# Delta rule: substitution on blocks of 16 with a compact merge, and the convolution's sums in PSUM

## Chip, cores and metric

The kernel runs on one core of a Trainium2 chip. The metric is the device time of one execution in microseconds (us); of the kernel before, three runs took 1975.92 to 1977.36 us, with a median of 1976.27 us.

## What is computed

The program is one step of a two-layer backbone for 128 context tokens and 512 latent tokens of width 1024. Layer 0 is a state-space mixer beside neighbourhood attention, layer 1 a bidirectional gated delta rule; both have an MLP. Only layer 1's mixer is touched. For each of 8 heads and each direction it does, on chunks of tokens:

```
qkv  = silu(dwconv(h @ w_in, conv_w))            # 5 taps along the tokens
q, k = q / |q| * dk**-0.5,  k / |k|
A    = tril(beta k k^T * decay, -1);   Tm = inv(I + A)
u, w = Tm @ (beta v),  Tm @ (beta k exp(gcum))
per chunk:  v_new = u - w @ S
            o     = (q exp(g)) @ S + (tril(q k^T) * decay) @ v_new
            S     = S exp(g_last) + (k exp(g_last - g))^T @ v_new
out  = (rmsnorm(o_fwd + o_bwd) * silu(z)) @ w_out
```

## The kernel before

All 640 tokens go together: 128 context tokens and 512 latent ones, in five chunks of 128 (chunk 0 is the context). Heads are handled in four pairs, P0 to P3, and one pair has both directions, so four units of 128 x 128 per chunk.

For a pair, `gdn_project` multiplies the normalised stream by six weight columns, m = 0 to 5 (k, k, q, q, v, v for the two heads). Each column is 2 halves x 8 x 3 = 48 matmuls of 320 columns (L205 to L207), 288 in a pair, and goes through `ev`: ScalarE copies it out of PSUM into `cb` (two buffers), the five taps are summed into `cv` (three buffers) by VectorE (L1322), a tanh and a last multiplication make it silu. After m = 1, `squares(0)`, `tok(0)` and `normalize` follow for the keys: squares summed on TensorE (L1272), a root in several small VectorE operations that begins at L1274 and ends at L182, transposition (L1299), multiplication (L1278), transposition back (L1285). After m = 3 come the squares of the queries, after m = 5 the transposed values. These use the PSUM tag `pc`, which hands out its banks in program order.

The squares stand in a tile of their own, `tsq`, with one buffer. The end of a chain (L1655, L1671) uses another tag with one buffer, `osq`, for the squares of its output and for the row of scales, which a DMA (`or`<-`osq`) writes out.

From m = 2 on, `gdn_group` runs once for each of the five chunks: decay factors (POOL L1376, ACT L1379), the product of the keys (L1394 and L1395), its evacuation (L1400), and DMAs that lay the 32 x 32 diagonal blocks of A as rows of `ub`, 80 rows of 1024. `gdn_blocks` inverts all 80 blocks at once by substitution, 31 steps of two VectorE operations (L1425 multiplies, L1427 subtracts).

`gdn_inverse` then builds the inverse of the 128 x 128 units. It spreads the blocks to block-diagonal tiles `gD` and `gTT` (POOL multiplies by a mask, L1453; VectorE transposes, L1454) and merges blocks of 32 to 64 and 64 to 128 with matmuls that have 128 rows and 32 or 64 columns (L1458). `gdn_chain` walks the chunks: t = 0 for the context, then t = 1 to 4, each with a step that depends on the state of the one before: TensorE L1615, VectorE L1620, TensorE L1625, ScalarE L1627, TensorE L1631/L1632 and L1643, VectorE L1646. It ends with L1655 to L1671.

In `odd` the program order is: project P0, P1, solve P0 (inverse and chain), P2, solve P1, P3, solve P2, then the projection of z and solve P3. A scheduler arranges each engine's instructions before the run into one fixed queue, from priorities (the chain and the inverse are the most urgent, then the substitution, then the groups) and its own estimates; DMAs are all issued by SP, in one queue. So an engine whose next instruction waits does nothing else. The gemm with `wouto` follows, and the scales of the last chain are used first at L1699.

Of the kernel before, what the change touches and what calls it, by code (L numbers as in the profile page):

```python
# [11 lines left out]
F32 = mybir.dt.float32  # L12
# [8 lines left out]
T = 640  # L21
# [127 lines left out]
class Build:  # L149
# [1098 lines left out]
    def gdn_project(self, pr, hn, P, first=None, mid=None):  # L1248
# [13 lines left out]
        def squares(ty):  # L1262

            p = self.ps("pc")
            for hh in range(2):
                for c0, c1 in ((0, 3), (3, 5)):
                    sq = P.tile([128, 4, 128], F32, name="tsq", bufs=1)
                    nc.scalar.activation(sq[:, :c1 - c0].rearrange("p a b -> p (a b)"),
                                         out[2 * ty + hh][:, 128 * c0:128 * c1], AF.Square)
                    for c in range(c0, c1):  # L1270
                        i = 2 * c + hh
                        nc.tensor.matmul(p[:, 2 * i:2 * i + 2], sq[:, c - c0], self.ones2, start=True, stop=True)  # L1272
            ssq = self.sp.tile([128, 10], F32, name="ssq", tag="ssq", bufs=2)
            V.tensor_scalar(ssq, p[:, 0:20:2], EPS, None, op0=AD)  # L1274
            return self.rsqrt(self.sp, ssq, 10, "l2n").rearrange("p (c h) -> p c h", h=2)
# [18 lines left out]
        def tok(ty):  # L1294
            for part in range(3):
                p = self.ps("pc")
                jobs = [(c, part) for c in range(1, 5)] if part < 2 else [(0, 0), (0, 1)]
                for i, (c, hh) in enumerate(jobs):
                    nc.tensor.transpose(p[:, 128 * i:128 * i + 128], out[2 * ty + hh][:, 128 * c:128 * c + 128], self.ident)  # L1299
                n = len(jobs)  # L1300
                pv = p.rearrange("p (a b) -> p a b", a=4)[:, :n]
                dst = ktok if ty == 0 else vtok
                if part < 2:
                    nc.scalar.activation(dst[part][:, 1:5], pv, AF.Copy)
                else:
                    for hh in range(2):
                        V.tensor_copy(dst[hh][:, 0], pv[:, hh])
        def ev(m, h, p):
# [9 lines left out]
            cv = self.tl([128, 642], "cv")  # L1318
            nc.scalar.activation(cv, cb[m][:, 0:642], AF.Identity, scale=cw[:, 0:1])  # L1319
            split = m > 3 and pr > 0  # L1320
            for t in range(1, 4 if split else 5):
                V.scalar_tensor_tensor(cv, cb[m][:, t:t + 642], cw[:, t:t + 1], cv, op0=M, op1=AD)  # L1322
            if split:
                cy = cb[m][:, 4:646]
                nc.scalar.activation(cy, cy, AF.Identity, scale=cw[:, 4:5])
                nc.gpsimd.tensor_tensor(cv, cv, cy, op=AD)
            th = cb[m][:, 0:642]
            nc.scalar.activation(th, cv, AF.Tanh)

            if m in (2, 3):  # L1330
                nc.scalar.activation(th, th, AF.Identity, bias=1.0)
                nc.gpsimd.tensor_tensor(cv[:, 0:128], th[:, 0:128], cv[:, 0:128], op=M)
                nc.gpsimd.tensor_tensor(cv[:, 128:T], th[:, 130:642], cv[:, 130:642], op=M)
            else:
                V.scalar_tensor_tensor(cv[:, 0:128], th[:, 0:128], 1.0, cv[:, 0:128], op0=AD, op1=M)
                V.scalar_tensor_tensor(cv[:, 128:T], th[:, 130:642], 1.0, cv[:, 130:642], op0=AD, op1=M)
# [78 lines left out]
    def gdn_blocks(self, pr, ub, P):  # L1415
# [3 lines left out]
        D = ub  # L1419
        V.memset(D.rearrange("p a b -> p (a b)")[:, 0:1024:33], 1.0)  # L1420
        tmp = P.tile([80, 256], F32, name="sbt", bufs=1)
        for j in range(31):
            n, m = 31 - j, j + 1
            t = tmp[:, :n * m].rearrange("p (a b) -> p a b", b=m)
            V.tensor_tensor(t, ub[:, j, j + 1:32].unsqueeze(2).to_broadcast([80, n, m]),  # L1425
                            D[:, j, 0:m].unsqueeze(1).to_broadcast([80, n, m]), op=ALU.mult)
            V.tensor_tensor(D[:, j + 1:32, 0:m], D[:, j + 1:32, 0:m], t, op=ALU.subtract)  # L1427
            if j < 30:
                tmp = P.tile([80, 256], F32, name="sbt", bufs=1)
# [4 lines left out]
    def gdn_inverse(self, pr, ud, dd, P):  # L1434
# [3 lines left out]
        cm = P.tile([128, 20, 32], F32, name="gcm")  # L1438
        nc.sync.dma_start(out=cm, in_=self.ap(dd, 0, [[32, 128], [4096, 20], [1, 32]]))
# [5 lines left out]
        mask = self.cst[:, 404:532].rearrange("p (b j) -> p b j", b=4).unsqueeze(1).to_broadcast([128, 2, 4, 32])  # L1445

        D = P.tile([128, 5, 4, 128], F32, name="gD")
        TT = P.tile([128, 5, 4, 128], F32, name="gTT", bufs=2)
        two = lambda t, c, d: t[:, c, 2 * d:2 * d + 2].rearrange("p u j -> p (u j)")
        for c in range(5):  # L1450
            for d, a, b in ((0, D, TT), (1, TT, D)):
                src = cm[:, 4 * c + 2 * d:4 * c + 2 * d + 2].unsqueeze(2).to_broadcast([128, 2, 4, 32])
                G.tensor_tensor(a[:, c, 2 * d:2 * d + 2].rearrange("p u (b j) -> p u b j", b=4), src, mask, op=ALU.mult)  # L1453
                V.transpose(two(b, c, d), two(a, c, d))  # L1454
        CH = [(c, hh) for c in range(5) for hh in range(2)]

        def mm(out, l, r, col):
            nc.tensor.matmul(out, l, r, start=True, stop=True, tile_position=(0, col))  # L1458

        def bank(n):  # L1460
            return self.ps("pb")[:, :320].rearrange("p (c h j) -> p c h j", c=5, h=2)


        p = bank(0)
        for c, hh in CH:
# [6 lines left out]
        pD, pT = bank(0), bank(0)
        for c, hh in CH:
            mm(pD[32:64, c, hh], TT[:, c, hh, 32:64], X[:, c, hh], 32)
            mm(pD[64:96, c, hh], TT[:, c, 2 + hh, 64:96], X[:, c, hh], 64)
        ACT.activation(D[32:64, :, 0:2, 0:32], pD[32:64], AF.Copy, scale=-1.0)
        ACT.activation(D[64:96, :, 2:4, 96:128], pD[64:96], AF.Copy, scale=-1.0)
        for c, hh in CH:
            for a in (0, 64):
                x, y = slice(a, a + 32), slice(a + 32, a + 64)  # L1480
                mm(pT[x, c, hh], X[:, c, hh], TT[:, c, hh, y], a)
                mm(pT[y, c, hh], X[:, c, hh], TT[:, c, 2 + hh, x], a + 32)
        for a in (0, 64):
            x, y = slice(a, a + 32), slice(a + 32, a + 64)
            ACT.activation(TT[x, :, 0:2, y], pT[x], AF.Copy, scale=-1.0)
            ACT.activation(TT[y, :, 2:4, x], pT[y], AF.Copy, scale=-1.0)

        x, y = slice(0, 64), slice(64, 128)
        Y = cm.rearrange("p (c h a) j -> p c h (a j)", c=5, h=2)
        parts = ((0, 4), (4, 5))  # L1490
        for c0, c1 in parts:
            p = self.ps("pb").rearrange("p (c h j) -> p c h j", c=4, h=2)
            for c in range(c0, c1):
                for hh in range(2):
                    mm(p[y, c - c0, hh], uo[:, 0, c, hh, 32:96], D[:, c, hh, x], 64)
                    mm(p[x, c - c0, hh], uo[:, 1, c, hh, 0:64], D[:, c, 2 + hh, y], 0)
            ACT.activation(Y[:, c0:c1], p[:, :c1 - c0], AF.Copy)
        for c0, c1 in parts:
            p = self.ps("pb").rearrange("p (c h j) -> p c h j", c=4, h=2)
            for c in range(c0, c1):  # L1500
                for hh in range(2):
                    mm(p[x, c - c0, hh], Y[:, c, hh], TT[:, c, hh, y], 0)
                    mm(p[y, c - c0, hh], Y[:, c, hh], TT[:, c, 2 + hh, x], 64)
            ACT.activation(TT[x, c0:c1, 0:2, y], p[x, :c1 - c0], AF.Copy, scale=-1.0)
            ACT.activation(TT[y, c0:c1, 2:4, x], p[y, :c1 - c0], AF.Copy, scale=-1.0)
        for c in range(5):
# [4 lines left out]
            else:  # L1511
# [8 lines left out]
                cR=("tsq", 1), cS=("cb", 2))  # L1520

    def gdn_chain(self, pr, pd, TT, P, roles, bank):
# [14 lines left out]
        def load(c):  # L1537

            if c not in held:
# [3 lines left out]
                held[c] = [a[k][:, i] for k in range(2) for i in range(4)]  # L1543
            return held[c]

        def prep(t):
# [9 lines left out]
            if t:  # L1556
# [9 lines left out]
                for u in range(4):  # L1566
                    nc.gpsimd.tensor_tensor(gq[:, u], gq[:, u], lds[u][2 + u % 2], op=M)
# [138 lines left out]
    def odd(self, hn, P, fillers, xd):  # L1706
# [22 lines left out]
        def blocks(pr, pd):  # L1729
            ub = P.tile([80, 32, 32], F32, name="ub", bufs=2)  # L1730
# [43 lines left out]
        zt = P.tile([128, 4, T], F32, name="gD")  # L1774
# [3 lines left out]
        for m in range(4):  # L1778
            o = ot[:, m] if m < 3 else P.tile([128, T], F32, name="gcm")
# [3 lines left out]
        zt = P.tile([128, 4, T], F32, name="gD")  # L1783
# [214 lines left out]
```

## Time and profile before

| | |
|---|---|
| median of three runs | 1976.27 us |
| profiled execution | 1976.35 us, of it 1974.1 us of span |
| TensorE busy | 1799.6 us (91%) |
| VectorE busy | 1290.8 us (65%) |
| ScalarE busy | 869.5 us (44%) |
| GpSimd busy | 760.8 us (39%) |

Layer 1's mixer lies between about 906 and 1475 us of the span. The digits of the page are tenths of busy time in slices of 49.4 us, so this stretch is slices 19 to 30. Times in the rows are microseconds from the start of the span.

### The profile page before, as it was taken

To read this page: it belongs to the slowest core of one execution; us is meant where nothing else is said; L and a number is where in the kernel's file an instruction comes from. 1 tells how busy PE (TensorE), PEld (TensorE's weight loads), DVE (VectorE), ACT (ScalarE), POOL (GpSimd) and SP (SyncE) were. 2 spreads that over 40 slices of the span, in tenths; PEclk is the share of its full clock that TensorE was granted. 3 is DMA by queue.
4 is the path that set the end of the run, shared out by engine and by line. 5 is a ranking of instruction groups with operands and counts; after the bars stand their busy time and mean duration, and the time that the engine had idled before them with its cause. 6 is when DMAs were issued, how large, how long until landed. Compare 5 with 4: busy or idle time off the path is not lost. (4 is left out here: it accounts for less than half of the span.)

```text
span 1974.1 us, 35755 instructions
## 1 busy us (share of the span) xinstructions
PE 1799.6 (91%) x13556; PEld 1698.3 (86%) x13556; DVE 1290.8 (65%) x2825; ACT 869.5 (44%) x1928; POOL 760.8 (39%) x609
## 2 busy tenths in 40 slices
PE   5889889998999999998877889889989899999998
PEld 3789677988999999998877788787878899999997
DVE  8999777369264544548589988774667927364553
ACT  4333356344244353536454455344324425344362
POOL 2622101442343433453455555522235334343451
PEclk9999999998999999998998999898989999999999
DMA  8446886524332222332576478758834122222231
GB/s 319 131 112 169 239 246 228 195 106 140 124 112 84 76 86 75 135 123 78 158 207 196 117 197 238 222 166 267 279 131 149 54 97 76 86 76 86 76 96 54
DMA packets 206985, 286.61 MB, mean 145 GB/s; under 512 B 54879, under 2 KB 138237, under 8 KB 206813
## 3 DMA queue, kind: packets, MB, share of 16 engines
q1 hardware_dynamic: 206812, 284.33, 45.6%
q8 instruction: 107, 1.75, 0.4%
q14 instruction: 66, 0.53, 0.1%
HBM read 228.87 MB, written 46.82 MB: 140 GB/s over the span
## 5 line engine op out<-in xcount | busy, mean ns | idle before, releaser
L196 POOL TENSOR_TENSOR wlo<-raw,whi 128x1024 fp32r<-128x1024 f32 (+1 forms) x153 | 360.8, 2361 | 512.6 <-ACT whi L194 466.6
L194 ACT ACTIVATE whi<-raw 128x1024 fp32r<-128x1024 f32 (+1 forms) x153 | 153.2, 1002 | 324.5 <-PE pg L206 146.6
L207 PE MATMUL pg<-hidh,wlo 128*128 128x320 f32 (+2 forms) x576 | 178.8, 311 | 0.5 <-POOL wlo L196 0.5
L205 PE MATMUL pg<-hidh,whi 128*128 128x320 f32 (+2 forms) x576 | 179.0, 311 | 0.0
L206 PE MATMUL pg<-hidl,whi 128*128 128x320 f32 (+2 forms) x576 | 178.9, 311 | 0.0
L205 PE MATMUL pg<-h10h,whi 128*128 128x320 f32 x472 | 158.9, 337 | 17.5 <-DVE cb L1722 6.5
L422 DVE SCALAR_TENSOR_TENSOR x<-pg,mod,x 128x128 f32<-128x128 f32 (+2 forms) x132 | 53.7, 436 | 179.5 <-PE pg L207 179.5
L206 PE MATMUL pg<-h10l,whi 128*128 128x320 f32 x472 | 155.9, 330 | 0.0
L207 PE MATMUL pg<-h10h,wlo 128*128 128x320 f32 x472 | 155.3, 329 | 0.0
L205 PE MATMUL pa<-hidh,whi 128*128 128x320 f32 x448 | 138.0, 310 | 0.5 <-ACT whi L194 0.5
L207 PE MATMUL pa<-hidh,wlo 128*128 128x320 f32 x448 | 138.4, 309 | 0.0
L206 PE MATMUL pa<-hidl,whi 128*128 128x320 f32 x448 | 138.2, 309 | 0.0
L422 DVE SCALAR_TENSOR_TENSOR x<-pa,mod,x 128x128 f32<-128x128 f32 (+2 forms) x108 | 43.8, 435 | 136.8 <-PE pa L207 136.8
L507 POOL TENSOR_TENSOR wq<-S,wq 128x512 fp32r<-128x512 f32 x52 | 71.3, 1371 | 114.4 <-ACT wq L506 114.4
L205 PEld LDWEIGHTS pg<-h10h,whi 128*128 128x128 f32 x472 | 95.9, 203 | 21.4 <-DVE cb L1722 7.2
L207 PEld LDWEIGHTS pg<-hidh,wlo 128*128 128x128 f32 x576 | 108.2, 188 | 1.6 <-POOL wlo L196 1.0
L205 PEld LDWEIGHTS pg<-hidh,whi 128*128 128x128 f32 x576 | 108.3, 188 | 0.9 <-issue 0.8
L206 PEld LDWEIGHTS pg<-hidl,whi 128*128 128x128 f32 x576 | 108.2, 188 | 0.4 <-DVE hidl L568 0.3
L1322 DVE SCALAR_TENSOR_TENSOR cv<-cb,cw,cv 128x642 f32<-128x642 f32 x90 | 94.6, 1052 | 9.8 <-ACT cv L1319 8.9
L206 PEld LDWEIGHTS pg<-h10l,whi 128*128 128x128 f32 x472 | 95.9, 203 | 0.6 <-issue 0.4
L207 PEld LDWEIGHTS pg<-h10h,wlo 128*128 128x128 f32 x472 | 95.6, 203 | 0.2
L205 PEld LDWEIGHTS pa<-hidh,whi 128*128 128x128 f32 x448 | 83.9, 188 | 2.0 <-ACT whi L194 1.2
(742 smaller groups left out, 5754.2 us busy)
## 6 DMA issues: line engine op xcount, KB each, us to landing
raw<-in_wff SPq DMA_DIRECT2D x104, 512.0 KB
mraw<-in_wmod SPq DMA_DIRECT2D x96, 512.0 KB
raw<-in_wino SPq DMA_DIRECT2D x33, 512.0 KB
rawx<-in_wff SPq DMA_DIRECT2D x24, 512.0 KB
raw<-in_wine SPq DMA_DIRECT2D x16, 512.0 KB
cka<-pd SPq DMA_DIRECT2D x28, 256.0 KB
ckb<-pd SPq DMA_DIRECT2D x28, 256.0 KB
s5g<-s5g SPq DMA_DIRECT2D x32, 164.0 KB
```

Source lines behind the costliest of these rows:

```text
L194: nc.scalar.activation(hi[:, :kt], raw[:, :kt], AF.Copy)
L196: (nc.vector if self.lov and self.nw % self.lov else nc.gpsimd).tensor_tensor(lo[:, :kt], raw[:, :kt], hi[:, :kt], op=ALU.subtract)
L205: nc.tensor.matmul(p[:, :n], hi[:, k], xh[:, s], start=(k == 0), stop=False)
L206: nc.tensor.matmul(p[:, :n], hi[:, k], xl[:, s], start=False, stop=False)
L207: nc.tensor.matmul(p[:, :n], lo[:, k], xh[:, s], start=False, stop=(k == kt - 1))
L422: nc.vector.scalar_tensor_tensor(x[m][:, s], p[:, ls], g, x[m][:, s], op0=ALU.mult, op1=ALU.add)
L507: (V if j % 2 else nc.gpsimd).tensor_tensor(t[:, 4:8], src, t[:, 0:4], op=SU)
L1322: V.scalar_tensor_tensor(cv, cb[m][:, t:t + 642], cw[:, t:t + 1], cv, op0=M, op1=AD)
```

## The change

Four things change in layer 1's mixer, and one of them brings a shared buffer.

The substitution works on blocks of 16: both halves of each block of 32 are handled by one operation, 15 steps of two operations on 30 to 128 elements a row instead of 31 steps on 31 to 256. It writes into a new tile, `ubd`, which GpSimd clears.

The inverse gets a level more, 16 to 32. Blocks stay compact (`gDc`, `gTc`: 128 rows, 32 columns a block); the matmuls take 32 or 64 rows as well as 32 or 64 columns of the array. The level 16 to 32 is 160 matmuls of 32 x 32 a pair, in two rounds of 80, with an evacuation between them. Masks and the block-wise transpositions go; the blocks are copied to their places by ScalarE.

The convolution is done in two parts, 128 tokens in SBUF and 512 in a bank of `pc`, with all sums and the last multiplication on VectorE. GpSimd and ScalarE had a share of these before.

The product of the queries with their decay (L1567) moves from GpSimd to VectorE, in two operations instead of four.

To make room, `squares` and the last pair's chain use the tag `osq` instead of `tsq`, `ub` has one buffer instead of two, and some later tiles take other tags. The core of the diff:

```diff
@@ squares
-                    sq = P.tile([128, 4, 128], F32, name="tsq", bufs=1)
+                    sq = self.tl([128, 5, 128], "osq")
@@ conv, called by ev
+            cv = self.tl([128, 642], "cv")
+            cl = self.ps("pc")
+            parts = ((cv[:, 0:128], 0), (cl, 130))
+            for o, c0 in parts:
+                nc.scalar.activation(o, x[:, c0:c0 + o.shape[1]], AF.Identity, scale=cw[:, 0:1])
+            for t in range(1, 5):
+                for o, c0 in parts[::-1]:
+                    V.scalar_tensor_tensor(o, x[:, c0 + t:c0 + t + o.shape[1]], cw[:, t:t + 1], o, op0=M, op1=AD)
...
@@ gdn_blocks
-        for j in range(31):
-            n, m = 31 - j, j + 1
...
+        D = P.tile([80, 32, 32], F32, name="ubd", bufs=1)
+        nc.gpsimd.memset(D, 0.0)
...
+        for j in range(15):
+            n, m = 15 - j, j + 1
+            sh = [80, 2, n, m]
...
@@ gdn_inverse
-                G.tensor_tensor(a[:, c, 2 * d:2 * d + 2].rearrange("p u (b j) -> p u b j", b=4), src, mask, op=ALU.mult)
-                V.transpose(two(b, c, d), two(a, c, d))
+        px = [bank() for d in range(2)]
+        for d in range(2):
+            for n in range(10):
+                for r in S:
+                    mm(px[d][r, n], Gc[r, d, n], Dc[r, d, n], r.start, r.start)
+            ACT.activation(Xc[:, d], px[d], AF.Copy)
...
+                    mm(px[d][r, n], Tc[r, d, n], Xc[r, d, n], r.start, r.start)
+            V.tensor_tensor(Dc[:, d], Dc[:, d], px[d], op=ALU.subtract)
+            V.transpose(fl(Tc[:, d]), fl(Dc[:, d]))
...
@@ gdn_chain
-                for u in range(4):
-                    nc.gpsimd.tensor_tensor(gq[:, u], gq[:, u], lds[u][2 + u % 2], op=M)
+                for d in range(2):
+                    V.tensor_tensor(gq[:, 2 * d:2 * d + 2], gq[:, 2 * d:2 * d + 2], lds[2 * d][8], op=M)
```

The fixed queues change with it. On TensorE, the place where P2's keys are normalised (`ktok`, L1285) stood among gemm matmuls (`pg`):

```order
L206 MATMUL pg<-h10l_8978,whi 128x320
L207 MATMUL pg<-h10h_8977,wlo 128x320
L1285 MATMUL pc<-cst,ktok 128x128 x4
L205 MATMUL pg<-h10h_8979,whi 128x320
L1285 MATMUL pc<-cst,ktok 128x128 x4
L206 MATMUL pg<-h10l_8980,whi 128x320
L207 MATMUL pg<-h10h_8979,wlo 128x320
```

Now the same place stands behind the end of P0's chain. L1689 is the chain's sum of squares, L1700 the transposition of its scales; L1272, L1299 and L1285 belong to P2's keys, L1394 to its five groups:

```order
L1689 MATMUL pa<-cst,osq 128x2 x5
L1601 MATMUL pa<-cka 128x128 x4
L1700 MATMUL pa<-cst,osc 10x128
L1272 MATMUL pc<-cst,osq 128x2 x3
L1299 MATMUL pc<-cst,cv 128x128 x4
L1272 MATMUL pc<-cst,osq 128x2 x2
L1299 MATMUL pc<-cst,cv 128x128 x4
L1272 MATMUL pc<-cst,osq 128x2 x3
L1299 MATMUL pc<-cst,cv 128x128 x2
L1272 MATMUL pc<-cst,osq 128x2 x2
L1285 MATMUL pc<-cst,ktok 128x128 x10
L1394 MATMUL pb<-khT 128x128 x10
```

P0's inverse and chain stand about one pair earlier among the gemm matmuls than before, and the keys of P2 follow the chain's end with no gemm matmul between them. From the second half of the chain's step t = 2 up to L1394 no L205 to L207 stands in the queue. Nearly the same stands once more at P1's chain and P3's keys.

On ScalarE, in the queue before, the last squares of P3 (`tsq`, the last row with L1268) stood ahead of the end of P0's chain (L1655):

```order
L1268 ACTIVATE tsq<-cv 128x256
L1510 ACTIVATE gTT<-gTT,gcol 128x128 x4
L1313 ACTIVATE cb<-pg 128x128
L1314 ACTIVATE cb<-pg 128x192
L1579 ACTIVATE ckd<-ckb,gkd 128x128 x2
L1655 ACTIVATE osq<-otok 128x640
L1562 ACTIVATE cgq<-cgq 128x512
L1655 ACTIVATE osq<-otok 128x640
```

Now the end of P0's chain (L1686, L1702) stands ahead of the first squares of P2's keys, all in one tag:

```order
L1686 ACTIVATE osq<-otok 128x640 x2
L1593 ACTIVATE cgq<-cgq 128x512
L1702 ACTIVATE osq<-pa 10x128
L1268 ACTIVATE osq<-cv 128x384
L1268 ACTIVATE osq<-cv 128x256
L1304 ACTIVATE ktok<-pc 128x512
L1268 ACTIVATE osq<-cv 128x384
L1304 ACTIVATE ktok<-pc 128x512
L1268 ACTIVATE osq<-cv 128x256
L1315 ACTIVATE cv<-cb,cw 128x128
```

P0's chain has moved ahead of two pairs' squares in this queue.

## Rows read from the trace of the kernel before

**Rows 1.** The page: sums by engine, and 40 slices.
```profile
PE 1799.6 (91%) x13556; PEld 1698.3 (86%) x13556; DVE 1290.8 (65%) x2825; ACT 869.5 (44%) x1928; POOL 760.8 (39%) x609
...
DVE  8999777369264544548589988774667927364553
```
**Rows 2.** Timeline of VectorE: start, duration, engine, line; the keys' normalisation.
```profile
962.87 1.56 DVE L1278 TENSOR_TENSOR ktok<-ktok,l2n_y 128x640 f32<-128x640 f32 x2
...
1021.56 1.55 DVE L1278 TENSOR_TENSOR ktok<-ktok,l2n_y 128x640 f32<-128x640 f32 x2
...
1102.21 1.54 DVE L1278 TENSOR_TENSOR ktok<-ktok,l2n_y 128x640 f32<-128x640 f32 x2
...
1182.24 2.10 DVE L1278 TENSOR_TENSOR ktok<-ktok,l2n_y 128x640 f32<-128x640 f32 x2
```
**Rows 3.** Busy time between these starts, then PEclk, DMA share, GB/s.
```profile
963.00:1022.00 59.00, 48.69 (x332) 47.40 (x333) 41.16 (x78) 31.82 (x72) 30.02 (x35) 0.94 0.82 235
1022.00:1102.00 80.00, 61.26 (x390) 58.97 (x390) 76.83 (x141) 35.96 (x76) 45.00 (x41) 0.91 0.55 159
1102.00:1182.00 80.00, 68.50 (x703) 65.47 (x702) 74.07 (x154) 43.57 (x102) 47.09 (x50) 0.92 0.64 173
1182.00:1475.00 293.00, 260.74 (x2539) 236.40 (x2537) 194.69 (x539) 119.72 (x278) 112.09 (x127) 0.93 0.72 221
```
**Rows 4.** Waits of TensorE, 1022 to 1475 us: total us, times, longest.
```profile
PE pc L1299 <- DVE cv L1336: 6.7, 2, 6.3
```
**Rows 5.** Timeline of TensorE: the last chain's scales.
```profile
1475.41 1.33 PE L1699 MATMUL pc<-cst,osc 128*128 128x128 f32 x5 [2.93 <-DVE osc L1666]
```
**Rows 6.** Groups by line, 900 to 1475 us: busy us, mean ns, idle before.
```profile
L1322 DVE SCALAR_TENSOR_TENSOR cv<-cb,cw,cv 128x642 f32<-128x642 f32 x90 | 94.6, 1052 | 9.8 <-ACT cv L1319 8.9 <-DMA pd<-khT 0.5
L1427 DVE TENSOR_TENSOR ub<-ub,sbt 80x31 f32<-80x31 f32 (+15 forms) x124 | 72.5, 584 | 1.6
L1425 DVE TENSOR_TENSOR sbt<-ub 80x31 f32<-80x31 f32 (+15 forms) x124 | 65.2, 526 | 3.0 <-DMA ub<-utd 1.2
...
L1400 DVE TENSOR_TENSOR gau<-pb,gbg 128x512 f32<-128x512 f32 x20 | 13.4, 681 | 5.5 <-ACT gbg L1379 4.9 <-DMA ckb<-pd 0.6
...
L1335 DVE SCALAR_TENSOR_TENSOR cv<-cb,cv 128x128 f32<-128x128 f32 x16 | 4.5, 284 | 1.6 <-ACT cb L1328 1.3
```
**Rows 7.** Groups of GpSimd, the same stretch.
```profile
L1567 POOL TENSOR_TENSOR cgq<-cgq,cka 128x128 f32<-128x128 f32 x64 | 31.5, 519 | 82.5 <-DVE cgl L1565 50.1 <-DMA cka<-pd 19.3 <-DVE ogn_t L180 7.6
```
**Rows 8.** Busy time of L1458 alone in two inverses (PE, PEld, PEclk).
```profile
1182.00:1218.00 36.00, 8.61 (x280) 6.49 (x280) 0.91 0.89 257
...
1277.00:1310.00 33.00, 7.33 (x280) 5.71 (x280) 1.00 0.54 159
```
**Rows 9.** Timeline of TensorE: runs of L1458 with 32 columns.
```profile
1189.87 0.45 PE L1458 MATMUL pb<-gD,guf 128*32 128x32 f32 x30
...
1199.40 1.02 PE L1458 MATMUL pb<-gcm,gTT 128*32 128x32 f32 x34
```
**Rows 10.** Timeline of TensorE: two gemm matmuls, and four matmuls of a chain.
```profile
1077.61 0.31 PE L206 MATMUL pg<-h10l,whi 128*128 128x320 f32 x1
1077.76 0.31 PE L207 MATMUL pg<-h10h,wlo 128*128 128x320 f32 x1
...
1310.32 1.06 PE L1643 MATMUL pa<-cR,ckd 128*128 128x128 f32 x8
```
**Rows 11.** Timeline: two steps of P2's chain.
```profile
1391.57 1.12 DVE L1620 SCALAR_TENSOR_TENSOR cR<-pa,gneg,ckb 128x128 f32<-128x128 f32 x4
...
1402.92 1.13 DVE L1620 SCALAR_TENSOR_TENSOR cR<-pa,gneg,ckb 128x128 f32<-128x128 f32 x4 [0.33 <-PE pa L1615]
```
**Rows 12.** Timeline of ScalarE: the end of P0's chain.
```profile
1220.68 0.73 ACT L1655 ACTIVATE osq<-otok 128x640 f32<-128x640 f32 x1
...
1259.61 0.27 ACT L1671 ACTIVATE osq<-pa 10x128 f32<-10x128 f32 x1 [1.20 <-PE pa L1669]
```
**Rows 13.** Timeline of VectorE: the root of P2's key squares begins.
```profile
1094.65 0.16 DVE L1274 TENSOR_SCALAR ssq<-pc 128x10 f32<-128x10 f32 x1
```

More of the change, by code (lines that the diff above doesn't have):

```diff
@@ L1317, in ev @@
             cw = self.cw[:, 6 * pr + m]
[L1318 to L1336, printed above, removed]
+            cv = conv(cb[m], cw)
             out[m] = cv
@@ L1455, in gdn_inverse @@
[L1455 to L1465, printed above, removed]
+        D64 = P.tile([128, 10, 64], F32, name="gD64")
+        G.memset(TT, 0.0)
+        G.memset(D64, 0.0)
+        fl = lambda t: t.rearrange("p n j -> p (n j)")
@@ new lines, in gdn_inverse, with mm, bank @@
+        V.transpose(fl(Tc[:, 0]), fl(Dc[:, 0]))
+        V.transpose(fl(Dc[:, 1]), fl(Tc[:, 1]))
+        def mm(out, l, r, row, col):
+            nc.tensor.matmul(out, l, r, start=True, stop=True, tile_position=(row, col))
+        def bank():
+            return self.ps("pb")[:, :320].rearrange("p (n j) -> p n j", n=10)
+        S = [slice(32 * k, 32 * k + 32) for k in range(4)]
+        px = [bank() for d in range(2)]
[4 more added lines that the diff above has]
+            ACT.activation(Xc[:, d], px[d], AF.Copy)
@@ new lines, in gdn_inverse @@
+        px = [bank() for d in range(2)]
+        for d in range(2):
+            for n in range(10):
+                for r in S:
+                    mm(px[d][r, n], Tc[r, d, n], Xc[r, d, n], r.start, r.start)
+            V.tensor_tensor(Dc[:, d], Dc[:, d], px[d], op=ALU.subtract)
+            V.transpose(fl(Tc[:, d]), fl(Dc[:, d]))
+        u2 = lambda d: slice(2 * d, 2 * d + 2)
+        ch = lambda t: t.rearrange("p (c h) j -> p c h j", h=2)
+        for d in range(2):
+            for r in S:
+                ACT.activation(TT[r, :, u2(d), r], ch(Tc[r, d]), AF.Copy)
+            for k in range(2):
+                r = S[2 * d + k]
+                ACT.activation(D64[r, :, 32 * k:32 * k + 32], Dc[r, d], AF.Copy)
@@ L1466, in gdn_inverse @@
+        p = bank()
+        for n in range(10):
+            c, hh = divmod(n, 2)
             for a in (0, 64):
                 x, y = slice(a, a + 32), slice(a + 32, a + 64)
-                mm(p[y, c, hh], uo[:, 0, c, hh, a:a + 32], D[:, c, hh, x], a + 32)
-                mm(p[x, c, hh], uo[:, 1, c, hh, a:a + 32], D[:, c, 2 + hh, y], a)
-        X = cm[:, :10].rearrange("p (c h) j -> p c h j", c=5)
+                mm(p[y, n], uo[x, 0, c, hh, a:a + 32], Dc[x, 0, n], a, a + 32)
+                mm(p[x, n], uo[y, 1, c, hh, a:a + 32], Dc[y, 1, n], a + 32, a)
@@ L1471, in gdn_inverse @@
+        X = Gc[:, 0]
         ACT.activation(X, p, AF.Copy)
[L1472 to L1478, printed above, removed]
+        pD, pT = bank(), bank()
+        for n in range(10):
+            mm(pD[32:64, n], Tc[32:64, 0, n], X[32:64, n], 32, 32)
+            mm(pD[64:96, n], Tc[64:96, 1, n], X[64:96, n], 64, 64)
@@ L1490, in gdn_inverse @@
[L1490 to L1505, printed above, removed]
+        Y = Xc.rearrange("p d n j -> p (d n j)").rearrange("p (n j) -> p n j", n=10)
```

83 lines of the change are left out of this document (54 added, 29 removed).

## The prediction

> **What bounds the kernel now.** I read the page first: TensorE is busy 91% of the span, and VectorE's digits rise to 9 and 8 only at the start and in slices 20 to 24, which is the delta rule [rows 1]. So the question is which engine sets the pace there. As milestones I take the normalisation of each pair's keys, because each pair passes it once, in order: 962.9, 1021.6, 1102.2 and 1182.2 us [rows 2]. The pairs are thus 58.7, 80.6 and 80.0 us apart. From the last to the use of the last chain's scales at 1475.4 us [rows 5] it is 293.2 us, and 499 us follow that the change does not touch. The busy table between these milestones shows VectorE at 77 and 74 us of 80 in the second and third stretch, against 41 of 59 in the first and 195 of 293 in the last, while TensorE has 61 and 68.5 of 80 [rows 3]. VectorE sets the pace in the second and third stretch; in the last TensorE is busy 261 of 293. The waits show how it reaches TensorE: once it stood 6.3 us for the last multiplication of a convolution [rows 4], work that had queued on VectorE.
>
> **What the change removes.** The substitution costs 72.5 + 65.2 = 137.7 us in 248 operations, 34.4 us a pair [rows 6]. 30 operations of at most 128 elements take its place. The nearest row is the 128x128 multiplication at 284 ns [rows 6]: 30 x 0.28 = 8.5 us; at the present mean of 555 ns it would be 16.7. I take 8.5, because that row has the size of the largest new operation, so 26 us a pair are saved (18 to 26). Masks and transpositions of the inverse go too; I count them as nothing, since the engines that wait for them wait in short pieces.
>
> **What it adds on VectorE.** A convolution is now four sums and a product in two parts. With 0.28 us for the 128 part and 0.68 for the part in PSUM (the row that reads 512 columns of PSUM, L1400) [rows 6] it is 5 x 0.96 = 4.8 us. Before, L1322 alone took 94.6 / 24 = 3.9 us a convolution [rows 6], with the last product on VectorE for 16 of 24. So it is about even, with 6 us a pair as upper bound. The query product, 64 x 519 ns on GpSimd [rows 7], becomes 32 operations of twice the size; between 0.28 (the 128x128 row) and 0.68 us (the 128x512 row) each, 2 to 5 us a pair on VectorE. The new level's subtractions and transpositions are six operations of 320 columns, at most 6 x 0.7 = 4 us. In all VectorE is relieved by some 12 to 20 us in a pair: the load of 77 and 74 is no longer what bounds.
>
> **What it adds on TensorE.** The inverse has 280 instructions with 8.6 and 7.3 us of busy time [rows 8], and 320 more are added. The runs of 32 columns go at 0.45 us for 30 up to 1.02 us for 34 instructions [rows 9], so 15 to 30 ns each: 320 are 4.8 to 9.6 us. I take 5 (several array parts are in use, as in the faster row), so 12.4 us an inverse. None of it is hidden: TensorE's queue is one.
>
> The Trainium skill (TensorEngine Tiling (Array Packing), Gotcha 1: PSUM Pressure) says that different row tiles cannot access the same PSUM bank simultaneously. Here the four row parts of a round write one bank. The faster row would then not hold for the new level, and no row here has matmuls with fewer than 128 rows that could agree or not. By it the four go in turn, as in the slower row; that is rival D.
>
> **What it moves: the step that decides.** Squares now share the one `osq` buffer with the end of a chain. In ScalarE's queue P0's chain end stands ahead of P2's squares, so these wait for the whole chain and for the DMA that writes the scales' row. In TensorE's queue nothing but the chain stands between. So there is a loop: the keys of P(k+2) wait for the chain of P(k), and the gemm cannot run far ahead, as `cv` has three buffers and `cb` two. The stretch without a gemm matmul, by rows:
>
> - the rest of the chain, from the second half of t = 2 to t = 4: two steps. A step took 1402.9 - 1391.6 = 11.4 us where the queues were least loaded [rows 11]. I take 21 us for two, as VectorE is emptier; 16 to 27.
> - the chain's end: two squares of 0.73 us [rows 12], the root, the row. The root routine of the keys took 1102.2 - 1094.7 = 7.6 us from its first operation to the multiplication [rows 2, 13]. With 1.5 for the squares, 1.3 for its matmuls (eight full ones took 1.06) [rows 10] and 1 for the small rest it is 11.5 us. Before it was 38.9 us with other work in between [rows 12]: 9 to 39.
> - the row's DMA: no row shows its landing. Between 0 and 4 us; I take 2.
> - P2's squares in four turns on one buffer, about 1 us each, and the root again, 7.6: 12 us.
> - normalisation, 1.6 us [rows 2], its banks, and the convolution of m = 2, 4.8 us and its two ScalarE passes, which must wait for a `pc` bank behind it and without which m = 4 cannot be taken from PSUM: 9 us; 6 to 14.
>
> The sum is 55.5 us. Outside it TensorE has 288 gemm matmuls that start 0.15 us apart [rows 10], so 43 us; an inverse, 12.4; and the first half of the chain, some 100 instructions at 0.12 us [rows 10], 12. That is 67 us at full rate, with almost no wait assumed. So a period is 122 us where it was 80.
>
> **The sum.** The chains of P0 and P1 now lie ahead of the last milestone, so the tail is shorter. It has 648 gemm matmuls, 97 us; two chains of about 230 instructions, 55; two inverses, 25; keys, groups and the modulation's small matmuls, 35 (an estimate, from the tail's 2539 instructions less those counted [rows 3]). That is 212 us, and at the share of busy time of the present tail, 261 of 293 (0.89), 238; with VectorE emptier I take 225 (205 to 245). The first distance I take as 62, for the convolutions behind the banks. Then 962.9 + 62 + 2 x 122 + 225 = 1493.9 us instead of 1475.4, so 18.5 us later. The profiled execution took 1976.35 us, 2.25 beyond its span and 0.08 above the median shown; with these, 1976.3 + 18.5 = 1994.8, so 1995 us. The two periods lose 83 us, and the tail gives 68 back.
>
> **Rivals.** A is the forecast, slower, 1995.
>
> B, faster: the freed VectorE shortens the chain. The point is the period: with 62 and 225 as above, 1475.4 is met at 112.8 us a period; each us below it counts twice. For it: VectorE was busy 93 to 96% of the time in just the stretches in which the chain's steps and roots were slow, and 38.9 us for a chain end whose own work is some 11 shows how much of it was queueing [rows 3, 12]. If a step takes 8 us, the end 9, and the tail follows with 215, the loop is 105: 962.9 + 62 + 210 + 215 = 1449.9, so 25.5 earlier, 1951 us. Against it: even then TensorE has no gemm to do for some 45 us, twice.
>
> C, no change: the period comes out at 111 to 115, by the same steps at the low end of the ranges; 1976.
>
> D: the row parts take turns. Each new instruction then costs 30 ns, and so do the other levels: 600 x 0.03 = 18 us instead of 12.4, or 5.6 more a pair, 22 in all; 2016 us.
>
> That the sharing does nothing, because the chain of P0 is done long before P2's keys, is a part of B: in TensorE's queue that chain ends behind all of P2's gemm matmuls up to m = 4, so I give it little.
>
> **Chances and range.** A 0.43, B 0.33, C 0.12, D 0.12. A change of 0.2% (4 us) is what a measurement here can tell from none; so faster 0.33, about the same 0.12, slower 0.55. A's own range is 1982 to 2020: a step between 8 and 13.5 us gives +-5 a period, the DMA, the banks and the tail about as much together. With 8 of 10 it reaches into B, whose middle is 1951, and to D: 1944 to 2032.
>
> **What would show it.** Right: in the changed profile VectorE is well under 80% from 1020 to 1180 us; the keys' multiplication comes at about 963, 1025, 1147 and 1269 us; ahead of the last two TensorE has a stretch of some 50 us in which it is busy for less than half, whose waits name `osq`, the chain's VectorE operations and the root; the granted clock, 0.91 and 0.92 in the stretches with waits now [rows 3], falls further there; the last chain's scales are used near 1494. B is right if these distances are under 113. D is right if a run of 32 x 32 matmuls costs 30 ns an instruction. I am wrong in the mechanism if squares of P2 run before P0's chain ends, or if TensorE waits elsewhere, as for the banks of the convolution.

## The result and the profile after

The changed kernel takes 2087.9 us (median of 4 runs, 2081.8 to 2092.4), 1.0558 times the kernel before (95% interval 1.0534 to 1.0582): 5.6% slower, some 111 us. The direction and the place were forecast, the size was not (1995 us, range to 2032).

The page of the changed kernel, sums and slices as in [rows 1] (with the row of TensorE's granted clock):

```profile
PE 1844.8 (88%) x14836; PEld 1737.0 (83%) x14836; DVE 1235.8 (59%) x2827; ACT 891.7 (43%) x2018; POOL 670.8 (32%) x503
...
PE   5789799989999999977869569668998899999998
...
DVE  8998876286463636386755454453545964545453
...
PEclk9999899989999999998869669679998999999999
```

VectorE was busy 55 us less than before and GpSimd 90 us less. In the mixer, slices 19 to 30, TensorE's digits fall to 5 and 6, and the clock's digits fall at the same slices. Before, TensorE's digits were 7 to 9 there, in this row of its page:

```profile
PE   5889889998999999998877889889989899999998
```

The keys' normalisations, against [rows 2], and the use of the last chain's scales, against [rows 5], in the timeline of the changed kernel:

```profile
963.03 1.56 DVE L1278 TENSOR_TENSOR ktok<-ktok,l2n_y 128x640 f32<-128x640 f32 x2
1041.13 1.56 DVE L1278 TENSOR_TENSOR ktok<-ktok,l2n_y 128x640 f32<-128x640 f32 x2
1190.26 1.56 DVE L1278 TENSOR_TENSOR ktok<-ktok,l2n_y 128x640 f32<-128x640 f32 x2
1347.88 1.56 DVE L1278 TENSOR_TENSOR ktok<-ktok,l2n_y 128x640 f32<-128x640 f32 x2
...
1593.74 1.33 PE L1730 MATMUL pc<-cst,osc 128*128 128x128 f32 x5 [1.68 <-DVE osc L1697]
```

The distances are 78.1, 149.1 and 157.6 us and the tail 245.9 us, where 58.7, 80.6, 80.0 and 293.2 stood and 62, 122, 122 and 225 were forecast. The busy table over them (columns as in [rows 3]):

```profile
963.00:1041.00 78.00, 56.90 (x349) 54.22 (x347) 59.72 (x142) 35.95 (x90) 28.99 (x36) 0.83 0.70 195
1041.00:1190.00 149.00, 110.55 (x1215) 103.30 (x1215) 77.52 (x219) 62.39 (x154) 32.33 (x39) 0.80 0.51 145
1190.00:1348.00 158.00, 115.14 (x1215) 107.89 (x1215) 74.85 (x222) 62.67 (x154) 32.34 (x39) 0.76 0.47 134
1348.00:1594.00 246.00, 208.22 (x2510) 189.59 (x2511) 123.78 (x328) 100.76 (x230) 53.55 (x40) 0.90 0.63 196
```

In the two long periods no engine is busy for more than 75%, and VectorE for about half: what sets the pace is a chain of waits. ScalarE's timeline at the end of P0's chain, answering to [rows 12], shows its link:

```profile
1165.20 0.72 ACT L1686 ACTIVATE osq<-otok 128x640 f32<-128x640 f32 x1
1167.34 0.74 ACT L1686 ACTIVATE osq<-otok 128x640 f32<-128x640 f32 x1 [1.42 <-PE pa L1689]
...
1178.10 0.27 ACT L1702 ACTIVATE osq<-pa 10x128 f32<-10x128 f32 x1 [5.73 <-PE pa L1700]
1179.69 0.52 ACT L1268 ACTIVATE osq<-cv 128x384 f32<-128x384 f32 x1 [1.32 <-DMA or<-osq]
```

P2's first square waits for the DMA that reads the row out of `osq`. TensorE's timeline of the same stretch, from the last gemm matmul ahead of the chain to the first ones behind it:

```profile
1142.20 0.31 PE L207 MATMUL pg<-h10h,wlo 128*128 128x320 f32 x1
1142.35 0.38 PE L1663 MATMUL pa<-cbc,cR 128*128 128x128 f32 x2
...
1165.97 1.28 PE L1689 MATMUL pa<-cst,osq 128*128 128x2 f32 x10 [1.71 <-ACT osq L1686]
...
1177.63 0.38 PE L1700 MATMUL pa<-cst,osc 128*10 128x128 f32 x1 [2.29 <-DVE osc L1697]
...
1191.14 2.49 PE L1285 MATMUL pc<-cst,ktok 128*128 128x128 f32 x10 [4.03 <-DVE ktok L1278]
...
1204.70 1.22 PE L1394 MATMUL pb<-khT 128*128 128x128 f32 x4 [6.17 <-DVE gau L1399]
...
1207.76 0.61 PE L205 MATMUL pg<-h10h,whi 128*128 128x320 f32 x1
1208.17 0.47 PE L206 MATMUL pg<-h10l,whi 128*128 128x320 f32 x1
1208.44 0.47 PE L207 MATMUL pg<-h10h,wlo 128*128 128x320 f32 x1
```

The waits add up to only part of the loss: behind this stall the gemm matmuls start 0.27 us apart, where [rows 10] has 0.15. The table over the stall (its edges lie about 1 us early), the stretch behind it, the rest of the way to the next one, and the next stall:

```profile
1141.50:1206.50 65.00, 36.33 (x207) 32.05 (x206) 29.18 (x93) 19.15 (x46) 9.92 (x12) 0.71 0.39 122
1206.50:1236.50 30.00, 20.48 (x463) 19.14 (x463) 12.50 (x32) 14.71 (x41) 7.69 (x9) 0.61 0.67 183
1236.50:1297.50 61.00, 54.09 (x540) 52.06 (x541) 33.73 (x95) 28.69 (x70) 14.74 (x18) 0.94 0.46 122
1297.50:1364.00 66.50, 40.43 (x217) 36.76 (x216) 28.29 (x93) 18.97 (x44) 9.86 (x12) 0.66 0.41 126
```

The granted clock is 0.71 in the stall and 0.61 in the 30 us behind it, so mostly at the lower of its two levels, 1.2 GHz, and 0.94 after.

To split the time between the milestones I summed TensorE's gaps between instructions (idle) and took half of the time in which it was busy at the lower clock (clock loss); the rest is counted as work at full clock. The clock loss is an estimate: it takes an instruction at the lower clock to last twice as long, where the gemm's starts went from 0.15 to 0.27 us. From the first milestone to the last chain's scales:

| us | length | idle | clock loss | work |
|---|---|---|---|---|
| before | 512 | 73 | 31 | 408 |
| after | 631 | 140 | 70 | 421 |
| after, 1041 to 1190 | 149.1 | 38.6 | 19.1 | 91.4 |
| after, 1190 to 1348 | 157.6 | 42.5 | 25.1 | 90.0 |

So of the added 118 us, 67 are idle, 39 clock loss and 12 to 13 work.

### The profile page after: what moved, and what is told of

It is laid out like the page before. It is cut to its first block, busy times and chain, and to the rows that moved or that the text cites. A ratio compares the mean times of both kernels' runs of the same rounds, so it can differ in the third digit from the quotient of the medians.

```text
span 2089.2 us, 38395 instructions
## 1 busy us (share of the span) xinstructions
PE 1844.8 (88%) x14836; PEld 1737.0 (83%) x14836; DVE 1235.8 (59%) x2827; ACT 891.7 (43%) x2018; POOL 670.8 (32%) x503
## 4 chain that ended last, share of the span: by engine, by line
PE 58%; DVE 17%; DMA 14%; issue 4%; SPq 3%; ACT 2%; POOL 1%; POOLq 0%; DVEq 0%; ACTq 0%
PE pg L205 7%; PE pg L207 7%; PE pg L206 7%; PE pa L206 4%; PE pa L205 4%; PE pa L207 4%; DMA mraw<-in_wmod 2%; DMA cgq<-gbd 2%; PE pg L525 2%; PE pg L526 2%; PE pg L527 2%; PE pa L525 2%; PE pb L525 2%; PE pa L526 2%; PE pb L526 2%
## 5 line engine op out<-in xcount | busy, mean ns | idle before, releaser
L196 POOL TENSOR_TENSOR wlo<-raw,whi 128x1024 fp32r<-128x1024 f32 (+1 forms) x153 | 355.0, 2323 | 647.3 <-ACT whi L194 578.0
L207 PE MATMUL pg<-hidh,wlo 128*128 128x320 f32 (+2 forms) x576 | 178.8, 311 | 0.6 <-POOL wlo L196 0.6
L205 PE MATMUL pg<-hidh,whi 128*128 128x320 f32 (+2 forms) x576 | 179.0, 311 | 0.0
L205 PE MATMUL pg<-h10h,whi 128*128 128x320 f32 x472 | 158.9, 337 | 6.5 <-DVE cb L1753 5.9
L207 PE MATMUL pg<-h10h,wlo 128*128 128x320 f32 x472 | 157.1, 333 | 0.0
L205 PE MATMUL pa<-hidh,whi 128*128 128x320 f32 x448 | 138.0, 310 | 0.7 <-ACT whi L194 0.7
L207 PE MATMUL pa<-hidh,wlo 128*128 128x320 f32 x448 | 138.4, 309 | 0.0
L422 DVE SCALAR_TENSOR_TENSOR x<-pa,mod,x 128x128 f32<-128x128 f32 (+2 forms) x108 | 43.9, 436 | 134.6 <-PE pa L207 134.6
L207 PEld LDWEIGHTS pg<-hidh,wlo 128*128 128x128 f32 x576 | 108.2, 188 | 1.6 <-POOL wlo L196 1.1
L205 PEld LDWEIGHTS pg<-hidh,whi 128*128 128x128 f32 x576 | 108.2, 188 | 0.9 <-issue 0.8
L205 PEld LDWEIGHTS pg<-h10h,whi 128*128 128x128 f32 x472 | 97.7, 207 | 7.9 <-DVE cb L1753 6.3
L207 PEld LDWEIGHTS pg<-h10h,wlo 128*128 128x128 f32 x472 | 97.2, 206 | 0.2
L205 PEld LDWEIGHTS pa<-hidh,whi 128*128 128x128 f32 x448 | 83.9, 188 | 2.1 <-ACT whi L194 1.3
L207 PEld LDWEIGHTS pa<-hidh,wlo 128*128 128x128 f32 x448 | 84.0, 188 | 0.4 <-issue 0.4
```

The source lines that it names most:

```text
L196: (nc.vector if self.lov and self.nw % self.lov else nc.gpsimd).tensor_tensor(lo[:, :kt], raw[:, :kt], hi[:, :kt], op=ALU.subtract)
L205: nc.tensor.matmul(p[:, :n], hi[:, k], xh[:, s], start=(k == 0), stop=False)
L207: nc.tensor.matmul(p[:, :n], lo[:, k], xh[:, s], start=False, stop=(k == kt - 1))
L422: nc.vector.scalar_tensor_tensor(x[m][:, s], p[:, ls], g, x[m][:, s], op0=ALU.mult, op1=ALU.add)
```

## Experiments

Each is timed against the kernel before on the same chip; the intervals, of 95%, are those of the ratios. A difference between two experiments is that of their medians, and where they ran on different chips the ratios give it to some 3 us; with the intervals of both it is uncertain by about 7 us.

**The sharing undone in the changed kernel.**

```diff
-                    sq = self.tl([128, 5, 128], "osq")
+                    sq = P.tile([128, 4, 128], F32, name="tsq", bufs=1)
...
-                cR=("osq", 1), cS=("cb", 2))
+                cR=("tsq", 1), cS=("cb", 2))
```

> The changed kernel with one thing undone: the squares of keys and queries have their own tile again, so they wait for no chain. Theory L (the loop of squares behind the chain through the one osq buffer makes the loss): the distances between the keys' normalisations fall from 149 and 158 us to 80 to 100, and the time to 1950 to 1995 us. Theory B (the loss comes from the convolution's bank and the longer inverse in TensorE's queue, and the sharing only orders what waits anyway): distances stay above 130 and the time above 2050 us.

2026.1 us, ratio 1.0228 (1.0202 to 1.0254): 62 us faster than the changed kernel, yet 47 slower than before. The second and third distances are 99 and 114 us (its milestones below), so distances and time lie between the two theories. The loop is the largest part of the loss, not all of it.

```profile
1037.88 1.56 DVE L1278 TENSOR_TENSOR ktok<-ktok,l2n_y 128x640 f32<-128x640 f32 x2
...
1136.64 1.55 DVE L1278 TENSOR_TENSOR ktok<-ktok,l2n_y 128x640 f32<-128x640 f32 x2
...
1251.03 1.56 DVE L1278 TENSOR_TENSOR ktok<-ktok,l2n_y 128x640 f32<-128x640 f32 x2
```

**The sharing alone, in the kernel before** (the same two lines, the other way).

> The kernel before with one thing done: the squares use the chain's osq buffer (and the last chain's result tile too), the rest as it was. Theory L: the time rises by 60 to 120 us to 2035 to 2100, with the keys of P2 and P3 normalised only behind a chain's end. Theory B: less than 20 us slower, under 1997.

2073.3 us, ratio 1.0461 (1.0433 to 1.0488): this one edit costs 94 us. The keys of P2 and P3 come 185 and 144 us after those ahead of them:

```profile
1021.62 1.55 DVE L1278 TENSOR_TENSOR ktok<-ktok,l2n_y 128x640 f32<-128x640 f32 x2
...
1206.61 1.56 DVE L1278 TENSOR_TENSOR ktok<-ktok,l2n_y 128x640 f32<-128x640 f32 x2
...
1350.33 1.56 DVE L1278 TENSOR_TENSOR ktok<-ktok,l2n_y 128x640 f32<-128x640 f32 x2
```

In ScalarE's timeline P2's first square stands behind the chain's row and waits for its DMA, as in the changed kernel:

```profile
1189.26 0.52 ACT L1268 ACTIVATE osq<-cv 128x384 f32<-128x384 f32 x1 [1.38 <-DMA or<-osq]
```

That is the loop, shown without any other part of the change.

**The row that ends a chain in a tile of its own** (changed kernel).

```diff
-        row = self.tl([128, T], "osq")[:10, :128]
+        row = P.tile([128, 128], F32, name="orow", bufs=1)[:10]
```

> The changed kernel, but the row of scales that ends a chain stands in a tile of its own; the squares still share the one osq buffer with the chain's squares. Theory L (the loop's length is the sum of what stands in it): the root of the chain's end, its row and the DMA, 12 to 15 us, leave the loop twice, so the time falls by 20 to 35 us to 2053 to 2068. Rival Q (the order of TensorE's queue alone holds the keys behind the chain): under 10 us faster, above 2078.

2078.9 us, ratio 1.0510 (1.0484 to 1.0537), 9 us faster: at the edge of the noise, and just inside what rival Q gives. In its trace P2's first square comes 3.9 us after the start of the chain's second, where it came 12.4 us after it, but TensorE's queue holds the chain's end and the keys close together all the same, and the periods are 147.4 and 144.2 us. The tail is longer, 253.4 us. What a link takes alone is not what its removal saves.

**The substitution and the compact inverse alone** (the kernel before, with `gdn_blocks` and `gdn_inverse` of the changed kernel and its tiles for them).

> The kernel before with the new substitution and the compact inverse alone; convolution, query product and squares as before. Theory L: VectorE is relieved by about 25 us a pair and TensorE gets 5 us a pair, so faster by 5 to 35 us: 1942 to 1972. Theory B: slower than before by over 20 us, above 1997, as the inverse's waits stand in TensorE's queue.

1997.9 us, ratio 1.0088 (1.0062 to 1.0113): 19 us slower, at the bound of theory B. The 120 operations take 43.9 us in its trace, 11 a pair, so VectorE is relieved nearly as forecast, and it is slower all the same.

**The same without the level from 16 to 32** (its 160 matmuls a pair, two copies and two subtractions are left out).

```diff
-        px = [bank() for d in range(2)]
...
-            V.tensor_tensor(Dc[:, d], Dc[:, d], px[d], op=ALU.subtract)
```

> The new substitution and compact inverse alone, with the level from 16 to 32 left out (its 160 matmuls a pair, two copies and two subtractions; the transpositions stay). Theory W (the level's work on TensorE made that kernel slower than the one before): 1998 falls by 12 to 25 us to 1973 to 1986. Theory N (the level hides in waits, and the queue order or the smaller buffers made it slower): within 8 us of 1998.

1969.4 us, ratio 0.9960 (0.9945 to 0.9975): the level costs 28.5 us (25 by the ratios), at or above the upper end of theory W, and more than its own TensorE time. The busy table of the inverse's line, with the level and without:

```profile
906.00:1501.00 595.00, 42.35 (x2400) 35.68 (x2400) 0.91 0.63 188
```

```profile
906.00:1475.00 569.00, 28.37 (x1120) 24.30 (x1120) 0.92 0.66 196
```

The difference is 14 us of busy time. The rest is not more waiting: over all of TensorE's work the idle time in these stretches is the same, 595.00 - 515.28 and 569.00 - 488.50 us, about 80 in both:

```profile
906.00:1501.00 595.00, 515.28 (x5588) 481.29 (x5586) 356.47 (x824) 288.58 (x647) 232.07 (x266) 0.91 0.63 188
```

```profile
906.00:1475.00 569.00, 488.50 (x4289) 457.43 (x4289) 364.31 (x816) 284.63 (x639) 230.24 (x263) 0.92 0.66 196
```

Of the 26 us by which these stretches differ, 8 are clock loss and 19 work, the level's 14 among them.

**VectorE relieved at no cost**: the kernel before with 2 of 31 steps of its substitution.

```diff
-        for j in range(31):
+        for j in range(14, 16):
...
```

> The kernel before, with 2 of the 31 steps of its substitution (29 steps are left out, so the inverse is not one), nothing else changed: VectorE is relieved by about 32 us a pair at no cost elsewhere. Theory V (VectorE sets the pace of the middle pairs): 40 us faster or more, under 1936. Theory N (another limit stands right behind VectorE, so its relief buys little): less than 20 us faster, above 1957.

1959.2 us, ratio 0.9907 (0.9889 to 0.9924): 19 us faster, just under theory N's bound of 20 and far from V's 40. VectorE falls to 58 us of 80 where it was 77 [rows 3], and TensorE's 64.3 is little more than the 61.3 of before:

```profile
1022.00:1102.00 80.00, 64.29 (x668) 61.34 (x667) 57.84 (x100) 42.26 (x95) 44.98 (x50) 0.91 0.66 182
```

So the 137.7 us of the substitution, less the 8.0 left of it, are worth 19 us. The run does not show the relief by itself: the queues are arranged anew in it too, with 668 instead of 390 of TensorE's instructions in this window, and its distances are 65.2, 66.1 and 116.7 us with a tail of 251.8.

**The convolution alone, in the kernel before.**

> The kernel before with the new convolution alone (two parts, the sums of 512 tokens in a PSUM bank). Theory L: VectorE gets up to 6 us a pair and the convolutions wait for banks; 0 to 25 us slower, 1976 to 2002. Theory B: over 30 us slower, above 2007.

1991.1 us, ratio 1.0054 (1.0035 to 1.0073), 12 us slower, as theory L has it. The waits of TensorE name its effect on the groups and the keys:

```profile
PE pc L1285 <- DVE ktok L1278: 8.8, 1, 8.8
...
PE pb L1393 <- DVE gau L1398: 7.1, 2, 5.2
```

**The same with both parts in SBUF.**

```diff
-            cl = self.ps("pc")
-            parts = ((cv[:, 0:128], 0), (cl, 130))
+            parts = ((cv[:, 0:128], 0), (cv[:, 130:642], 130))
```

> The kernel before with the new convolution in two parts, all of it on VectorE and ScalarE, but with both parts in SBUF as before, so that it needs no PSUM bank. Theory P (the wait for a bank of pc costs the 12 us): back to 1974 to 1984. Theory W (the extra VectorE operations cost it): 1988 or more.

2014.2 us, ratio 1.0179 (1.0156 to 1.0201): slower still by 23 us. So theory P's time is not met, and theory W's is. VectorE's sums take longer here, 124.8 us in this trace against 69.9 + 42.4 with the PSUM part. But the sums of 128 columns, which stand in SBUF in both runs, grew more (from 441 to 557 ns on average) than those of 512 (from 742 to 790), and TensorE's waits for the modulation's weights (L281, 16.3 us where they were 2.8) and for squares (L1272, 20.6 where they were 13.4) grew too. The run changes more than the bank, so what the wait for a bank costs stays open.

**The old convolution in the changed kernel** (the code of before in `ev`; sharing kept).

> The changed kernel with the convolution of before (in SBUF, GpSimd and ScalarE taking their share); squares still share osq. Theory G (the convolution's bank puts the five groups' products in one block behind the normalisation, inside the loop): TensorE's wait for the groups' evacuation falls from 31 us to under 10, and the time by 20 to 45 us to 2043 to 2068. Rival: the convolution adds only its own work, 5 to 15 us faster, 2073 to 2083.

2085.6 us, ratio 1.0530 (1.0503 to 1.0557): 2 us faster, not to be told from none. The wait of the groups does shrink, as theory G has it, from 31.0 us in the changed kernel (first row) to 5.2 (second row), but other waits fill the same loop, in the rows behind them:

```profile
PE pb L1394 <- DVE gau L1399: 31.0, 8, 6.7
...
PE pb L1396 <- DVE gau L1401: 5.2, 1, 5.2
...
PE pc L1285 <- DVE ktok L1278: 21.6, 2, 10.8
PE pa L1658 <- DVE cR L1653: 15.1, 9, 3.5
```

Theory G is wrong in its time: while the loop stands, no cost of the convolution can be told from the noise.

**Substitution, inverse and the query product on VectorE.**

> The new substitution and inverse and the query product on VectorE, with the convolution of before and squares in a tile of their own: beside the run with the substitution and inverse alone (1998) it prices the move of the product. Theory S (VectorE has room now and GpSimd is relieved): 1990 to 2000. Rival (the product now stands in VectorE's queue ahead of the chain's steps): 2003 to 2020.

1990.1 us, ratio 1.0059 (1.0038 to 1.0080): in theory S's range. Beside the run without the move it is 8 us faster (6 by the ratios), which the two intervals do not tell from none.

**The old substitution with the compact inverse, no level.**

> A candidate: the kernel before with its own substitution on 32 and the compact inverse without the level from 16 to 32; the triangle's mask is eight GpSimd products of 32 rows in place of the 20 of 128. Theory W (the level's work on TensorE is what made the compact inverse lose; without masks and block-wise transpositions it wins): 1955 to 1972. Theory N (VectorE and GpSimd work that goes there buys nothing): 1973 to 1985.

1992.3 us, ratio 1.0060 (1.0037 to 1.0083): slower, against both theories. Taking out the 20 mask products of 128 rows (L1453, 16.4 + 18.7 us before) and the block-wise transpositions bought nothing here. Up to the last chain's scales its trace is no slower (1473.6 us, before 1475.4), but by then 1648 of the mixer's gemm matmuls had run where 1702 had before; the loss is behind them, 517 us where 499 stood. Why is not settled.

**Matmuls that nobody reads, in the wait at the chain's end** (changed kernel, P0 and P1).

```diff
+        if pr < 2:
+            for i in range(20):
+                nc.tensor.matmul(p[:, 256:512], self.ident, otok[1][:, i % 4:i % 4 + 2].rearrange("p a b -> p (a b)"), start=True, stop=True)
```

> The changed kernel with 20 more matmuls of 256 columns, which nobody reads, in TensorE's wait between the squares and the scales at the end of P0's and of P1's chain (where it stood 8 to 10 us idle). Theory K (half of what the stalls cost is the low clock behind them): the granted clock of the stretches that follow rises and the time falls by 5 to 20 us in spite of the added work. Rival: the added matmuls only delay what follows, 0 to 10 us slower.

2111.4 us, ratio 1.0666 (1.0639 to 1.0692), 24 us slower (21 by the ratios), more than the rival had. The added matmuls took 10.7 us at a clock partly low, and delayed the chain's row; the stretches behind them have the clock they had:

```profile
1173.00:1183.50 10.50, 10.50 (x42) 8.65 (x40) 1.96 (x9) 0.00 (x0) 0.00 (x0) 0.83 0.00 0
1183.50:1206.00 22.50, 11.88 (x57) 9.76 (x56) 12.50 (x35) 6.44 (x13) 1.38 (x2) 0.65 0.27 79
1206.00:1236.00 30.00, 20.29 (x387) 18.79 (x387) 13.65 (x29) 14.59 (x43) 11.77 (x18) 0.61 0.74 201
```

It says nothing on what the clock would give back without the stalls, as the waits behind it stayed.

**The query product alone, in the kernel before.**

```diff
-                for u in range(4):
-                    nc.gpsimd.tensor_tensor(gq[:, u], gq[:, u], lds[u][2 + u % 2], op=M)
+                for d in range(2):
+                    V.tensor_tensor(gq[:, 2 * d:2 * d + 2], gq[:, 2 * d:2 * d + 2], lds[2 * d][8], op=M)
```

> A candidate: the kernel before with the query product alone moved to VectorE, in two operations. Beside the run with the substitution it was worth 8 us. Theory S (GpSimd's share of the product stood in the chain's way): 4 to 10 us faster than before, 1967 to 1973. Rival (VectorE is full here, so the product delays the chain): 0 to 12 us slower.

1975.8 us against 1979.5 for the kernel before beside it, ratio 0.9974 (0.9958 to 0.9990): faster by 0.1 to 0.4%. It is the one part of the change that gained when it stood alone, and by little.

## Why the prediction was wrong

**Right: the loop.** The squares of P2 and P3 waited for the chains of P0 and P1 and for the row's DMA. One buffer, put into the kernel before, costs 94 us; taken out of the changed kernel, it gives back 62 of the 111. Its terms: the rest of the chain took 1165.2 - 1142.4 = 22.8 us (21 forecast), the chain's end to the row's start 12.9 (11.5), the row and its DMA 1.6 (2), squares to multiplication 10.6 (12), and from there to the gemm 17.5 (9). The stall is 65.4 us, not 55.5; the second one, 66.5 us in the table, has the same parts. The last term is the one that was mis-sized, and it names the wrong work: it was worked out from the convolution of m = 2, where the trace has TensorE wait for the evacuation of the groups' products (L1399), 6.2 us at one place. That wait was in none of the terms.

**Wrong: "67 us at full rate, with almost no wait assumed".** This is the step that failed. With the stalls of the table, 65.0 and 66.5 us, the rest of the period took 84 us the first time and 91 the second. In the 91, from 1206.5 to 1297.5 us, there are 63.1 us of work (67 forecast), 16.4 of idle and 11.5 of clock loss. The two longest waits of TensorE in it are for the subtraction of the inverse's new level (L1483) and for a convolution (L1322):

```profile
PE pb L1465 <- DVE gDc L1483: 4.4, 1, 4.4
PE pc L1299 <- DVE cv L1322: 3.9, 1, 3.9
```

I had named the low clock as a sign to look for and gave it no term in the sum; its loss is 70 us between the milestones, 31 of which were there before. The rest's excess of 17 and 24 us and the stall's of 10 and 11 make the miss of 27 and 36 us in the two periods. With 16 us in the first distance and 21 in the tail, the last chain's scales come at 1593.7 us, 100 us behind the 1493.9 of the forecast.

**Wrong in the same way: the first distance and the tail.** The first distance is 78 instead of 62, with 21 us of idle and 8 of clock loss, though no squares wait for a chain there. Most of it is the convolution's: alone in the kernel before it makes this distance 80.5 us, and with the old convolution the changed kernel has 68.3. The tail is 246 instead of 225, with 38 of idle and 18 of clock loss; its work is 190, less than the 212 that were counted, so what failed is the choice of 225 below the 238 that the old share of busy time gave. That sharing alone leaves a tail of 225.5 us, and the changed kernel one of 245.9, points to the other parts.

**Wrong: VectorE as the engine that sets the pace.** I read 93 to 96% of busy time as the bound. A relief of 32 us a pair, with new work nowhere, bought 19 us in all. [rows 3] held a bound on that: TensorE was idle for 80.00 - 61.26 and 80.00 - 68.50, some 30 us in those two stretches, and by the split above the low clock cost it 11 more. With the same work of TensorE in them, no relief of VectorE could shorten them by more. So the gain in rival B's price was not there, and its chance of 0.33 was too high; no period of the changed kernel came under 113.

Part of that busy time was probably not VectorE's own work either. In the run with 2 of 31 steps, two multiplications of nearly the same size take 1.76 and 0.42 us; the long one lies under an operation of GpSimd, the short one does not:

```profile
1097.85 1.76 DVE L1425 TENSOR_TENSOR sbt<-ub 80x255 f32<-80x255 f32 x1
...
1100.10 0.42 DVE L1425 TENSOR_TENSOR sbt<-ub 80x256 f32<-80x256 f32 x1
```

```profile
1096.92 2.40 POOL L196 TENSOR_TENSOR wlo<-raw,whi 128x1024 fp32r<-128x1024 f32 x1 [4.40 <-ACT whi L194]
```

In the kernel before, the 92 of the substitution's 248 operations that overlap one of GpSimd took 936 ns on average, the other 156 took 331; all 37 that took more than 800 ns overlap one. If all had taken 331 the substitution would be 82 us and not 137.7, an estimate. No run tests this by itself.

**Mis-sized: the level from 16 to 32.** Its matmuls cost less than forecast, not more: all of the inverse's are 42.7 us in the changed kernel, 10.7 a pair, where 12.4 were forecast. In the changed kernel's timeline of TensorE a run of 80 takes

```profile
1063.49 0.89 PE L1465 MATMUL pb<-gDc,gGc 32*32 32x32 f32 x80
```

so 11 ns each, where 15 were taken, and rival D's 30 does not occur in it: four row parts of the array, each with columns and partitions of its own, write one bank at that rate. The rule of the Trainium skill (TensorEngine Tiling (Array Packing), Gotcha 1: PSUM Pressure) that different row tiles cannot access the same PSUM bank simultaneously shows no price here; no run gives each of the four a bank of its own to compare. But the level as a whole costs 25 to 28 us where its busy time is 14. TensorE is not idle for longer with it; 8 us are clock loss, and the few us beyond are not traced.

**Even, as forecast:** the substitution (38.4 us for 120 operations in the changed kernel's trace, 9.6 a pair; 8.5 forecast). The convolution alone, whose work on VectorE was taken as about even with 6 us a pair as bound, costs 12 us in all; on VectorE its sums and products took 69.7 + 47.9 + 16.0 + 9.6 = 143.2 us in the changed kernel, 6.0 a convolution where 4.8 were forecast. The parts do not add up: sharing 94, convolution 12 and substitution with product 12 make 118, near the 111 measured, but without the sharing convolution, substitution and product together cost 47, and with it the convolution's cost cannot be told from none. Why the three together cost twice the sum of their separate prices stays open. One part has no run of its own: `ub` has one buffer instead of two, and in the changed kernel VectorE's first step of the substitution stands 14.9 us for the DMA that fills it, where 1.2 us stood before [rows 6]. What the low clock would give back alone stays open too.

## What to carry to other kernels

A tile tag with one buffer is an order: before sharing one, list who holds it, how long, and what stands behind the waiting instruction in each fixed queue. When a stall is priced, price the lower clock in it and behind it too, from rows at the lower clock in the same trace: here the added clock loss, 39 us, was over half of the added idle time, 67 us. An engine that is busy 95% of a stretch is not thereby the bound: the idle time of the engine that it is said to hold up limits what its relief can be worth, and cutting its work in an experiment shows it before a change is built on it.

## What the runs showed of the hardware

VectorE's sums of 512 columns took 742 ns on average with the accumulator in PSUM, and 790 ns with it in SBUF; as the sums of 128 columns, in SBUF both times, went from 441 to 557 ns between the same two runs, the difference is not to be put down to the place. Operations of the substitution on VectorE took 936 ns where one of GpSimd overlapped them and 331 ns where none did. The recorded instructions of 32 x 32 matmuls on four diagonal parts of the array started 11 ns apart into one PSUM bank. Behind a stall of 65 us, in which the granted clock was 0.71, it was 0.61 for 30 us, and gemm matmuls started 0.27 us apart instead of 0.15.
